# Layer 0's two gate chunks computed as 512-wide products

## The chip, the cores and the metric

The kernel runs on one core of a Trainium2 chip. The metric is the device time of one execution in microseconds (us); the median of three timed runs of the kernel before is 246.11 us (246.09 to 246.35). The profile is of a further execution of its own.

## The reference

Two layers run over 256 positions of width 1024, followed by a final RMSNorm. Each layer projects the normed input through one wide matrix, runs three kinds of heads on slices of the projection, multiplies each result by its own SiLU gate, and projects back:

```python
hn = rms_norm(x, norm_gain)
proj = jnp.einsum('bsd,de->bse', hn, w_in)
a_q, a_k, a_v, a_g, b_x, b_g, c_q, c_k, c_v, c_g = jnp.split(proj, _in_split_points(), axis=-1)
...
y_a = dilated_attention(qa, ka, va) ... * jax.nn.silu(a_g)
y_b = rg_lru_branch(b_x, ...) * jax.nn.silu(b_g)
y_c = stick_breaking_attention(qc, kc, vc) ... * jax.nn.silu(c_g)
y = jnp.concatenate([y_a, y_b, y_c], axis=-1)
return x + jnp.einsum('bse,ed->bsd', y, w_out)
```

The change concerns `c_g` (the stick-breaking gate) and `b_g` (the recurrent gate) of the first layer: 256 columns of the projection each.

## The kernel before

**Precision.** The inputs are float32. Each operand of a projection is split into a rounded part and a rest, both in a reduced type: `whi`, `wlo` for a chunk of weights and `xh`, `xl` for the input, which lie side by side in `xx`, so that the 512 columns of one `xx[:, k]` are the 256 positions of `xh` and then those of `xl`. A product is taken as three: hi·hi, hi·rest and rest·hi. The split of weights is ScalarE's copy (L115, `whi`) and VectorE's subtraction (L117, `wlo`), four of each per chunk of 256 columns, prefetched from a ring of DMA tiles `st`.

**Two forms of the projection.** `proj_b` (L326) makes a chunk in two halves of 128 columns, each a contraction over eight blocks k. A chunk that is not in `PAIRED` goes through `mm3` (L225): 16 products of 256 columns with `whi` and 8 with `wlo` for each half, both halves summed into one PSUM bank. A chunk in `PAIRED` makes, for each half, eight 512-wide products of `whi` with `xh` and `xl` at once (L344) and eight 256-wide ones of `wlo` with `xh` (L341), in a bank for each half; its two 256-column parts are then added, ScalarE copying one to `low` (L347) and VectorE adding the other (L349). Before, layer 0 has only the two chunks of the dilated gate (`CH_AG`, `CH_AG + 1`) in that form; layer 1 has nearly all.

**A gate in layer 0.** The norm's factor is not yet in `xx` there, so `silu` (L428) first multiplies the sum by the row `rb` (L413, through `scaled`), then takes the sigmoid on ScalarE (L84, through `tab`) and multiplies on VectorE (L435). `emit_y` (L437) multiplies a head group's result by its gate and splits that into `yh` (ScalarE, L441) and `yl` (VectorE, L442) for the output projection.

**Order.** TensorE runs in the order in which the code is written (`manual_schedule`). On the other engines a scheduler places the instructions when the program is built, and each engine then runs its list strictly in order. Around the change TensorE does, in layer 0: the stick-breaking gate's chunk (`CH_CG`), the transposes of the first four dilated heads' probabilities (L489), the first half of the recurrent gate's chunk (`CH_BG`), then `third`: the gates' products of the recurrence (`lru_gates`, L601), the values of the stick-breaking and of the first dilated heads (L453) and the score products of the other four dilated heads (`dil_scores`, L542); then the second half of `CH_BG`, the two dilated gate chunks and the output projection.

**PSUM.** The pool `pp` has three banks for projections, the pool `at` four banks named `s`, and `yp` one. Both rings give out the bank that was given out longest ago and is free again. So the four score banks of `dil_scores(4)` follow three banks of transposes and the two banks of `lru_gates`: the third and the fourth score bank are those that ScalarE's sigmoids read, `rt` from the one and `it` from the other (L605, shown as L84 with `rt<-s` and `it<-s`). One of the three `pp` banks is held by the first dilated heads' values (L670) until they are multiplied by their gate (`emit_y` at L688), so the dilated gate's four half chunks alternate between the other two: the second chunk's first half needs the bank of the first chunk's first half, which is free after its addition (`agf<-pp,low`, L349).

Of the kernel before, what the change touches and what calls it, by code (L numbers as in the profile page):

```python
# [42 lines left out]

CH_AV, CH_CV, CH_CQ, CH_CK, CH_BX, CH_CG, CH_BG, CH_AG, CH_O = 0, 2, 3, 4, 7, 10, 11, 12, 14
CH_AQ, CH_AK = (5, 8), (6, 9)
PAIRED = ((CH_AG, CH_AG + 1), (CH_CQ, CH_CK, CH_AQ[0], CH_AK[0], CH_BX, CH_AQ[1], CH_AK[1], CH_CG, CH_BG, CH_AG, CH_AG + 1))


@with_exitstack
def trunk_kernel(ctx: ExitStack, tc: tile.TileContext, x, first_x, first, wpack, prm_d, gatew, gains, consts, rope, out):  # L50
# [12 lines left out]
    def bank(pool, tag):  # L63
        return pool.tile([P, 512], F32, name=tag, tag=tag)

    def scr(w):
        return wk.tile([P, 512], F32, name="scr", tag="scr", bufs=SCR)[:, 0:w]
# [9 lines left out]
    def table(name, behind=()):  # L77
        load = act.preload_act_table_set(name)  # L78
        for u in (*loaded["users"], *behind):
            dep(load, u)  # L80
        loaded["load"], loaded["users"] = load, []

    def tab(*a, **k):
        i = dep(act.activation(*a, **k), loaded["load"])  # L84
        loaded["users"].append(i)
        return i

    def v2(a, n=2):
        return a.rearrange("p (b t) -> p b t", b=n)
# [34 lines left out]
    def ask(l, c, ahead=AHEAD):  # L124
        last = order.index((l, c)) + ahead
        while pending and order.index(pending[0]) <= last:
            i = pending.pop(0)
            ready[i] = load_chunk(*i)

    def weights(l, c, ahead=AHEAD):  # L130
        ask(l, c, ahead)
        return ready.pop((l, c))
# [87 lines left out]
    def mm3(ps, lhs, rhs, ks, first, last, skip=False):  # L220
        lh, ll = lhs
        rh, rl = rhs
        seq = [(a, b, k) for a, b in ((lh, rh), (lh, rl), (ll, rh)) for k in ks]
        for i, (a, b, k) in enumerate(seq):
            pe.matmul(ps, a(k), b(k), start=first and i == 0, stop=last and i == len(seq) - 1,  # L225
                      skip_group_check=skip)
# [84 lines left out]
    for l in range(L):  # L311
# [5 lines left out]
        def y_half(h):  # L317
            ys[h] = [sb.tile([P, 4, S], F32R, name=n, tag=f"{n}{h}") for n in ("yh", "yl")]
# [7 lines left out]
        def proj_b(c, mid=None, to=None, sc=1.0):  # L326
            pair = c in PAIRED[l]
            hi, lo = [a.rearrange("p (k c) -> p k c", c=256) for a in weights(l, c, AHEAD - 1 if mid else AHEAD)]
            if pair:
                flat = None if to is not None else scr(512)  # L330
                to = [v2(flat)[:, b, :] for b in range(2)] if to is None else to
            else:
                flat = bank(pp, "pp")
            for b in range(2):
                cs = slice(b * P, b * P + P)
                if pair:
                    ps = last["bank"] = bank(pp, "pp")
                    seq = [(b ^ i, k) for i in range(2) for k in range(NK)]
                    for i, (is_lo, k) in enumerate(seq):
                        if is_lo:  # L340
                            pe.matmul(ps[:, 0:S], lo[:, k, cs], xh[:, k, :], start=i == 0, stop=i == len(seq) - 1,  # L341
                                      skip_group_check=True)
                        else:
                            pe.matmul(ps, hi[:, k, cs], xx[:, k].rearrange("p h t -> p (h t)"), start=i == 0,  # L344
                                      stop=i == len(seq) - 1, skip_group_check=True)
                    low = wk.tile([P, S], F32, name="low", tag="low", bufs=2)
                    act.activation(low, ps[:, S:2 * S], AF.Copy, scale=sc)  # L347
                    if sc == 1.0:
                        dve.tensor_add(to[b], ps[:, 0:S], low)  # L349
                    else:  # L350
                        dve.scalar_tensor_tensor(to[b], ps[:, 0:S], sc, low, ALU.mult, ALU.add)
                else:
                    mm3(flat[:, b * 256:(b + 1) * 256], [lambda k, a=a: a[:, k, cs] for a in (hi, lo)],
                        [lambda k, a=a: a[:, k, :] for a in (xh, xl)], range(NK), b == 0, True, True)
                if b == 0 and mid:
                    mid()
                    ask(l, c)
            return flat

        def proj_to(dst, c, mid=None, sc=1.0):  # L360
            if l > 0 and c in PAIRED[l]:
                proj_b(c, mid, [dst[:, b, :] for b in range(2)], sc)
            else:
                scaled(dst, proj_b(c, mid), sc)

        def rows(ps, b=2):
            return v2(ps, b), rb.rearrange("p (o t) -> p o t", o=1).broadcast_to([P, b, S])
# [42 lines left out]
        def scaled(dst, ps, sc=1.0):  # L410
            if l == 0:
                a, b = rows(ps)
                dve.scalar_tensor_tensor(dst, a, sc, b, ALU.mult, ALU.mult)  # L413
            else:
                act.activation(dst, v2(ps), AF.Copy, scale=sc)
# [4 lines left out]
        def tables():  # L420
            if l == 0:
                nc.sync.dma_start(out=rp, in_=rope)
            nc.sync.dma_start(out=gw_t, in_=gatew[:, l, :])

        if l > 0:
            tables()

        def silu(dst, ps):  # L428
            sg = v2(scr(512))
            src = v2(ps)  # L430
            if l == 0:
                src = v2(scr(512))
                scaled(src, ps)
            tab(sg, src, AF.Sigmoid)
            dve.tensor_mul(dst, src, sg)  # L435

# [128 lines left out]
        def dil_transposes(h0):  # L565
            if h0 == 0:
                a = sb.tile([P, 1024], F32, name="pa", tag="yh1")
                b = sb.tile([P, 512], F32, name="pb", tag="yl1")
                to, heads = (a[:, 0:512], a[:, 512:1024], b), by_head(a, b)
            else:  # L570
                to, heads = turned_tile()
            turned(prob, h0, range(3), to)
            return heads
# [7 lines left out]
        bg = sb.tile([P, 2, S], F32, name="bg", tag="bg")  # L581
        cg = sb.tile([P, 2, S], F32, name="cg", tag="cg")
# [74 lines left out]
        rotated(CH_AK[1], kT, 4, "k1")  # L657
        split_qk(4, ("q0", "ag"))
        table(SIGM)
        cg_ps = proj_b(CH_CG)  # L660
        pts = dil_transposes(0)
        silu(cg, cg_ps)


        y_half(0)

        def third():
# [2 lines left out]
            y_c["y"] = values(va, pts, 0, bank(pp, "pp"))  # L670
            y_c["s"] = dil_scores(4)

        silu(bg, proj_b(CH_BG, third))
        y_half(1)
        table(LN_EXP)
        lru_scan()
# [2 lines left out]
        ps = None  # L679
        if CH_AG in PAIRED[l]:  # L680
            agf = sb.tile([P, 2, S], F32, name="agf", tag="cg")
            proj_b(CH_AG, None, [agf[:, b, :] for b in range(2)])
            ps = agf.rearrange("p b t -> p (b t)")
        dil_softmax(y_c["s"])
        ps = proj_b(CH_AG) if ps is None else ps
        table(SIGM)
        silu(ag[:, 0:2, :], ps)
        emit_y(y_c["y"], ag[:, 0:2, :], 4, 2)  # L688
        seeded = proj_b(CH_AG + 1)
        silu(ag[:, 2:4, :], seeded)  # L690
        if CH_AG + 1 in PAIRED[l]:
            seeded = last["bank"]
# [161 lines left out]
```

## Time and profile before

| | us |
|---|---|
| median of the timed runs | 246.11 |
| time of the profiled execution | 246.06 |
| span of its trace | 244.2 |
| TensorE busy, matmuls | 236.2 (97%) |
| TensorE busy, weight loads | 206.6 (85%) |
| VectorE busy | 200.0 (82%) |
| ScalarE busy | 174.4 (71%) |
| GpSimd busy | 10.5 (4%) |

Matmuls overlap in the trace, so a matmul's own duration is longer than its distance from the next; the steps of the chain of waits give the distance. Of the engines' instructions, too, the next one starts a little before the end of the one ahead. A name such as `whi<-st` says what an instruction writes and reads; L115 is line 115 of the kernel before. Times in the views count from the start of the span.

### The profile page before, as it was taken

To read this page: it belongs to the slowest core of one execution; us is meant where nothing else is said; L and a number is where in the kernel's file an instruction comes from. 1 tells how busy PE (TensorE), PEld (TensorE's weight loads), DVE (VectorE), ACT (ScalarE), POOL (GpSimd) and SP (SyncE) were. 2 spreads that over 40 slices of the span, in tenths; PEclk is the share of its full clock that TensorE was granted. 3 is DMA by queue.
4 is the path that set the end of the run, shared out by engine and by line. 5 is a ranking of instruction groups with operands and counts; after the bars stand their busy time and mean duration, and the time that the engine had idled before them with its cause. 6 is when DMAs were issued, how large, how long until landed. Compare 5 with 4: busy or idle time off the path is not lost.

```text
span 244.2 us, 4576 instructions
## 1 busy us (share of the span) xinstructions
PE 236.2 (97%) x1651; PEld 206.6 (85%) x1651; DVE 200.0 (82%) x480; ACT 174.4 (71%) x384; POOL 10.5 (4%) x43
## 2 busy tenths in 40 slices
PE   8799999999999999999999999999999999999991
PEld 4588999999999798878888888888888878887881
DVE  3694699999999889999495585999999986997362
ACT  3677987919597689994673674876669867998143
POOL 0017200002000000000000000000010000000000
PEclk9999999999999999999999999999999999999999
DMA  6989988565846843068448288615470771000022
GB/s 193 377 254 390 384 268 291 190 205 177 240 152 207 272 153 105 1 195 320 175 134 273 88 289 268 199 44 177 171 214 7 226 282 63 31 0 0 3 75 97
DMA packets 14037, 43.89 MB, mean 180 GB/s; under 512 B 1728, under 2 KB 3008, under 8 KB 14016
## 3 DMA queue, kind: packets, MB, share of 16 engines
q1 hardware_dynamic: 13248, 42.43, 51.9%
q0 software_dynamic: 192, 0.52, 0.8%
q10 hardware_dynamic: 576, 0.66, 0.7%
q8 instruction: 13, 0.21, 0.4%
q14 instruction: 8, 0.07, 0.1%
HBM read 42.03 MB, written 1.05 MB: 176 GB/s over the span
## 4 chain that ended last, share of the span: by engine, by line
PE 94%; DMA 3%; DVE 1%; SPq 0%; ACT 0%; issue 0%; DVEq 0%
PE pp L225 34%; PE pp L344 20%; PE pp L341 10%; PE s L225 9%; PE s L181 4%; PE s L489 3%; DMA st<-first 3%; PE y L453 2%; PE pp L383 2%; PE s L542 2%; PE pp L181 2%; PE s L469 1%; PE y L225 1%; PE pp L453 1%; PE s L601 1%; PE s L273 1%
## 5 line engine op out<-in xcount | busy, mean ns | idle before, releaser
L117 DVE TENSOR_TENSOR wlo<-st,whi 128x512 fp32r<-128x512 f32 x128 | 81.8, 684 | 7.5 <-ACT whi L115 6.9
L115 ACT ACTIVATE whi<-st 128x512 fp32r<-128x512 f32 x130 | 72.5, 627 | 9.0 <-DMA st<-w_pack 3.4
L344 PE MATMUL pp<-xx,whi 128*128 128x512 f32 x208 | 50.8, 393 | 0.0
L344 PEld LDWEIGHTS pp<-xx,whi 128*128 128x128 f32 x208 | 37.8, 188 | 7.6 <-DVE q L349 0.3
L225 PE MATMUL pp<-xx,whi 128*128 128x256 f32 x288 | 38.2, 285 | 0.0
L225 PEld LDWEIGHTS pp<-xx,whi 128*128 128x128 f32 x288 | 35.8, 191 | 0.8 <-issue 0.3
L341 PEld LDWEIGHTS pp<-xx,wlo 128*128 128x128 f32 x208 | 26.9, 191 | 1.6 <-ACT scr L84 0.3
L341 PE MATMUL pp<-xx,wlo 128*128 128x256 f32 x208 | 28.0, 284 | 0.0
L225 PE MATMUL pp<-xx,wlo 128*128 128x256 f32 x144 | 20.2, 283 | 0.0
L84 ACT ACTIVATE pr<-scr,mn 128x128 f32<-128x128 f32 (+1 forms) x32 | 14.1, 443 | 6.6 <-DVE mn L549 6.6
L225 PEld LDWEIGHTS pp<-xx,wlo 128*128 128x128 f32 x144 | 18.6, 192 | 0.0
L78 ACT ACT_TABLE_LOAD x13 | 16.7, 1283 | 1.9 <-PEq L847 1.7
L347 ACT ACTIVATE low<-pp 128x256 f32<-128x256 f32 x26 | 9.4, 373 | 8.8 <-PE pp L344 8.0
L225 PE MATMUL pp<-whi,yh 128*128 128x512 f32 (+1 forms) x48 | 14.1, 382 | 0.0
L225 PE MATMUL pp<-wlo,yh 128*128 128x512 f32 (+1 forms) x48 | 13.7, 372 | 0.0
L225 PE MATMUL pp<-whi,yl 128*128 128x512 f32 (+1 forms) x48 | 13.6, 371 | 0.0
L181 PE MATMUL s<-whi,xx 128*128 128x512 f32 (+1 forms) x36 | 9.6, 384 | 1.8 <-ACT xx L161 1.7
L225 PEld LDWEIGHTS pp<-whi,yl 128*128 128x128 f32 x48 | 8.6, 188 | 1.6
L225 PEld LDWEIGHTS pp<-wlo,yh 128*128 128x128 f32 x48 | 8.6, 188 | 1.6
L225 PEld LDWEIGHTS pp<-whi,yh 128*128 128x128 f32 x48 | 8.3, 188 | 1.6 <-issue 0.3
L549 DVE CUSTOM_DVE_ANT_0 scr<-s,con 128x128 f32<-128x128 f32 (+1 forms) x32 | 9.2, 350 | 0.0
L181 PEld LDWEIGHTS s<-whi,xx 128*128 128x128 f32 x36 | 6.0, 197 | 3.3 <-ACT xx L161 2.5
(189 smaller groups left out, 372.3 us busy)
## 6 DMA issues: line engine op xcount, KB each, us to landing
st<-w_pack SPq DMA_DIRECT2D x66, 512.0 KB, 5.3
st<-first SPq DMA_DIRECT2D x7, 512.0 KB, 7.0
xres<-x_in SPq DMA_DIRECT2D x4, 256.0 KB, 7.5
gw_t<-gate_w SPq DMA_DIRECT2D x2, 256.0 KB, 6.8
gn<-gains SPq DMA_DIRECT2D x2, 256.0 KB, 5.9
xs<-xc POOLq DMA_DIRECT2D x4, 128.0 KB, 3.8
gf<-gains SPq DMA_DIRECT2D x2, 256.0 KB, 5.4
out<-st ACTq DMA_DIRECT2D x2, 192.0 KB, 2.0
```

What stands on the lines that cost most here:

```text
L78: load = act.preload_act_table_set(name)
L84: i = dep(act.activation(*a, **k), loaded["load"])
L115: split[l, c] = act.activation(h, part, AF.Copy)
L117: dve.tensor_sub(r, part, h.bitcast(F32))
L181: pe.matmul(ps[t][:, c0:c1], a[:, k, t * P:(t + 1) * P], b, start=k == 0 and all(m[0] is not ps for m in seq[:i]), stop=k == NK - 1 and al ...
L225: pe.matmul(ps, a(k), b(k), start=first and i == 0, stop=last and i == len(seq) - 1, skip_group_check=skip)
L341: pe.matmul(ps[:, 0:S], lo[:, k, cs], xh[:, k, :], start=i == 0, stop=i == len(seq) - 1, skip_group_check=True)
L344: pe.matmul(ps, hi[:, k, cs], xx[:, k].rearrange("p h t -> p (h t)"), start=i == 0, stop=i == len(seq) - 1, skip_group_check=True)
L347: act.activation(low, ps[:, S:2 * S], AF.Copy, scale=sc)
L453: pe.matmul(y[hr, p * 128 + o:p * 128 + 256], vt[:, s0, hs], wts[i][s0], start=s0 == 0, stop=s0 == 1)
L489: pe.transpose(tp[:, i * P:(i + 1) * P], tiles[h0 + h][:, j * P:(j + 1) * P], ident)
L549: dve.tensor_tensor_reduce(xs[:, cs], sps[h][:, cs], nmask[:, cs], -0.125, 3e38, ALU.add, ALU.min, mn[:, t:t + 1])
```

## The change

The two gate chunks of layer 0 join `PAIRED`, and their halves are added straight into the gates' own tiles `cg` and `bg`, from which `silu` then reads.

```diff
-PAIRED = ((CH_AG, CH_AG + 1), (CH_CQ, CH_CK, ...
+PAIRED = ((CH_CG, CH_BG, CH_AG, CH_AG + 1), (CH_CQ, CH_CK, ...
...
+        def home(tile_):
+            return [tile_[:, b, :] for b in range(2)] if l == 0 else None
+
         def silu(dst, ps):
             sg = v2(scr(512))
-            src = v2(ps)
+            src = dst if ps is None else v2(ps)
             if l == 0:
-                src = v2(scr(512))
-                scaled(src, ps)
+                ps, src = src, v2(scr(512))
+                scaled(src, ps.rearrange("p b t -> p (b t)"))
             tab(sg, src, AF.Sigmoid)
             dve.tensor_mul(dst, src, sg)
...
-        cg_ps = proj_b(CH_CG)
+        cg_ps = proj_b(CH_CG, None, home(cg))
...
-        silu(bg, proj_b(CH_BG, third))
+        silu(bg, proj_b(CH_BG, third, home(bg)))
```

Per chunk, TensorE's 48 products of 256 columns become 16 of 512 and 16 of 256. ScalarE gets two copies more (L347) and VectorE two additions more (L349); the product with `rb` now reads `cg` or `bg` instead of PSUM. Each half has a bank of its own. Behind the edited lines all line numbers are 3 higher after the change (L435 becomes L438, and so on).

How the rows of the other engines move shows at three places. VectorE, from the split of the second dilated key tile (`qk`) to the first gated result; before:

```order
L528 TENSOR_TENSOR qk_1038<-k_965,qk_1038 128x512
L117 TENSOR_TENSOR wlo<-st,whi 128x512 x4
L413 SCALAR_TENSOR_TENSOR scr<-pp,rb 128x512
L117 TENSOR_TENSOR wlo<-st,whi 128x512 x3
L435 TENSOR_TENSOR cg<-scr 128x512
L117 TENSOR_TENSOR wlo<-st,whi 128x512
L615 TENSOR_TENSOR it<-it,xc 128x512
L439 TENSOR_TENSOR scr<-y,cg 128x512
```

And the same stretch after the change:

```order
L531 TENSOR_TENSOR qk_1038<-k_965,qk_1038 128x512
L349 TENSOR_TENSOR cg<-pp,low 128x256
L117 TENSOR_TENSOR wlo<-st,whi 128x512 x4
L349 TENSOR_TENSOR cg<-pp,low 128x256
L117 TENSOR_TENSOR wlo<-st,whi 128x512
L413 SCALAR_TENSOR_TENSOR scr<-cg,rb 128x512
L117 TENSOR_TENSOR wlo<-st,whi 128x512
L438 TENSOR_TENSOR cg<-scr 128x512
L117 TENSOR_TENSOR wlo<-st,whi 128x512 x2
L349 TENSOR_TENSOR bg<-pp,low 128x256
L618 TENSOR_TENSOR it<-it,xc 128x512
L442 TENSOR_TENSOR scr<-y,cg 128x512
```

Two additions and one subtraction of weights now stand ahead of the product with `rb` (L413) that feeds the sigmoid.

ScalarE from the copies of the transposed probabilities (`pa`, `pb`) to the dilated gate's first `low`, before (the first `scr<-scr` is the sigmoid of `cg`, the second that of `bg`):

```order
L490 ACTIVATE pb<-s 128x512
L84 ACTIVATE scr<-scr 128x512
L115 ACTIVATE whi<-st 128x512
L84 ACTIVATE rt<-s,prm_t 128x256 x2
L84 ACTIVATE it<-s,prm_t 128x256 x2
L84 ACTIVATE th<-rt,nc_286 128x256 x2
L441 ACTIVATE yh<-scr 128x512
L115 ACTIVATE whi<-st 128x512 x4
L84 ACTIVATE scr<-scr 128x512
L78 ACT_TABLE_LOAD
L84 ACTIVATE av<-rt,c_285 128x256 x2
L347 ACTIVATE low<-pp 128x256
```

And from the sigmoid of `cg` on after it:

```order
L84 ACTIVATE scr<-scr 128x512
L115 ACTIVATE whi<-st 128x512 x2
L347 ACTIVATE low<-pp 128x256
L84 ACTIVATE rt<-s,prm_t 128x256 x2
L84 ACTIVATE it<-s,prm_t 128x256 x2
L84 ACTIVATE th<-rt,nc_286 128x256 x2
L444 ACTIVATE yh<-scr 128x512
L347 ACTIVATE low<-pp 128x256
L115 ACTIVATE whi<-st 128x512 x3
L84 ACTIVATE scr<-scr 128x512
L78 ACT_TABLE_LOAD
L84 ACTIVATE av<-rt,c_285 128x256 x2
```

Between the sigmoid of `cg` and `rt` stand two copies of weights and one `low` instead of one copy of weights; ahead of the sigmoid of `bg` a `low` takes the place of one copy of weights.

VectorE again, where the first dilated heads' result is gated, ahead of the output projection; before:

```order
L442 TENSOR_TENSOR yl<-scr,yh 128x512
L435 TENSOR_TENSOR ag<-scr 128x512
L585 MEMSET bxp 128x2x3
L439 TENSOR_TENSOR scr<-pp,ag 128x512
L349 TENSOR_TENSOR scr<-pp,low 128x256 x2
```

After the change:

```order
L445 TENSOR_TENSOR yl<-scr,yh 128x512
L438 TENSOR_TENSOR ag<-scr 128x512
L117 TENSOR_TENSOR wlo<-st,whi 128x512
L442 TENSOR_TENSOR scr<-pp,ag 128x512
L349 TENSOR_TENSOR scr<-pp,low 128x256 x2
```

A subtraction of weights stands where the small memset was.

More of the change, by code (lines that the diff above doesn't have):

```diff
@@ L45 @@
 CH_AQ, CH_AK = (5, 8), (6, 9)
-PAIRED = ((CH_AG, CH_AG + 1), (CH_CQ, CH_CK, CH_AQ[0], CH_AK[0], CH_BX, CH_AQ[1], CH_AK[1], CH_CG, CH_BG, CH_AG, CH_AG + 1))
+PAIRED = ((CH_CG, CH_BG, CH_AG, CH_AG + 1), (CH_CQ, CH_CK, CH_AQ[0], CH_AK[0], CH_BX, CH_AQ[1], CH_AK[1], CH_CG, CH_BG, CH_AG, CH_AG + 1))
 @with_exitstack
```

## The prediction

> **What bounds the kernel now.** I read the page first: how busy each engine is, then the chain of waits.
>
> ```profile
> PE 236.2 (97%) x1651; PEld 206.6 (85%) x1651; DVE 200.0 (82%) x480; ACT 174.4 (71%) x384; POOL 10.5 (4%) x43
> PE 94%; DMA 3%; DVE 1%; SPq 0%; ACT 0%; issue 0%; DVEq 0%
> ```
>
> TensorE (PE) is busy for 97% of the span and makes up 94% of the chain that ends last. So a shorter TensorE stream shortens the kernel one for one, as long as nobody makes TensorE wait; and whoever does adds his lateness one for one. Next I read the chain in order of time around the two gates (start, length, what, and the number of matmuls).
>
> ```profile
> 60.12 14.59 PE pp L225 x120
> 74.71 1.31 PE s L489 x12
> 76.02 2.86 PE pp L225 x24
> 78.88 1.02 PE s L601 x16
> ...
> 82.66 1.36 PE s L542 x38
> 84.02 3.06 PE pp L225 x24
> 87.08 1.84 PE pp L344 x8
> 88.92 1.91 PE pp L341 x16
> ...
> 102.29 5.48 PE pp L225 x24
> ```
>
> The stick-breaking gate's chunk is the last 48 of the 120 matmuls in the first row. The recurrent gate's halves are the rows at 76.02 and 84.02; between them lie the recurrence's gate products at 78.88 and, last, the scores of four heads at 82.66. No other engine shows in this stretch: TensorE never waited. What I need, then, is how near the others come to being late. These are VectorE's rows in the order of time (start, length, line, what; in brackets the idle time ahead):
>
> ```profile
> 75.23 0.68 DVE L528 TENSOR_TENSOR qk<-k,qk 128x512 fp32r<-128x512 f32 x1
> 75.83 2.49 DVE L117 TENSOR_TENSOR wlo<-st,whi 128x512 fp32r<-128x512 f32 x4
> 78.24 0.68 DVE L413 SCALAR_TENSOR_TENSOR scr<-pp,rb 128x512 f32<-128x512 f32 x1
> ...
> 81.85 0.68 DVE L615 TENSOR_TENSOR it<-it,xc 128x512 f32<-128x512 f32 x1
> 82.45 0.68 DVE L439 TENSOR_TENSOR scr<-y,cg 128x512 f32<-128x512 f32 x1
> 83.83 0.69 DVE L442 TENSOR_TENSOR yl<-scr,yh 128x512 fp32r<-128x512 f32 x1 [0.70 <-ACT yh L441]
> ...
> 87.12 0.69 DVE L413 SCALAR_TENSOR_TENSOR scr<-pp,rb 128x512 f32<-128x512 f32 x1 [0.38 <-PE pp L225]
> ...
> 91.13 0.69 DVE L617 TENSOR_TENSOR scr<-av 128x512 f32<-128x512 f32 x1 [0.31 <-ACT av L84]
> 91.74 0.42 DVE L349 TENSOR_TENSOR agf<-pp,low 128x256 f32<-128x256 f32 x1
> ...
> 100.09 0.69 DVE L439 TENSOR_TENSOR scr<-pp,ag 128x512 f32<-128x512 f32 x1
> ```
>
> VectorE works without a gap from 75.23 to the product with rb at 78.24: whatever is put ahead of that product delays it. ScalarE in the same stretch:
>
> ```profile
> 79.02 0.63 ACT L84 ACTIVATE scr<-scr 128x512 f32<-128x512 f32 x1 [0.64 <-DVE scr L413]
> 79.55 0.61 ACT L115 ACTIVATE whi<-st 128x512 fp32r<-128x512 f32 x1
> 80.07 0.82 ACT L84 ACTIVATE rt<-s,prm_t 128x256 f32<-128x256 f32 x2
> 80.79 0.83 ACT L84 ACTIVATE it<-s,prm_t 128x256 f32<-128x256 f32 x2
> ...
> 88.26 0.61 ACT L84 ACTIVATE scr<-scr 128x512 f32<-128x512 f32 x1
> 88.89 1.28 ACT L78 ACT_TABLE_LOAD   x1
> 90.19 0.91 ACT L84 ACTIVATE av<-rt,c 128x256 f32<-128x256 f32 x2
> 91.00 0.36 ACT L347 ACTIVATE low<-pp 128x256 f32<-128x256 f32 x1
> ```
>
> The sigmoid at 79.02 is what the reader should look at. ScalarE stood idle for 0.64 us because VectorE's L413 was not done, with rt and it queued behind. it ends at 80.79 + 0.83 = 81.62 and frees the bank that the fourth head's scores are written to; TensorE comes there at 82.66. The slack is 1.04 us.
>
> **What TensorE saves.** The 120 matmuls at 60.12 begin behind another kind of product; such a restart costs 3.06 - 2.86 = 0.20 us by the two rows of the recurrent gate. So a half of 24 products takes (14.59 - 0.20)/5 = 2.88 us. A half in the new form takes eight wide products, 1.84 us by the row at 87.08, and eight narrow ones, half of the 1.91 at 88.92: 2.80 us. That saves 0.08 per half, **0.33 us** in four halves (unrounded 0.083 each). Three of the halves, 0.25 us, lie ahead of the scores.
>
> One rule bears on this. The Trainium skill ("TensorE: Matmul & The Clock Gate", section "Back-to-back issue gap") gives an isolated matmul's gap as N/2.4 + 2.5 ns, an estimated 216 ns for 512 columns and 109 for 256; by it a half would go from 24 x 109 = 2.62 us to 2.60, and the whole change would save TensorE 0.07 us, with a time 0.26 us above mine. The rows show 1.84/8 = 230 and 1.91/16 = 119 ns, so this trace does not bear the page out, and the sum goes by the rows.
>
> **What VectorE and ScalarE add ahead of the scores.** Nothing upstream moves, so VectorE ends the split of the key tile as before and is free at 75.83 (an instruction starts 0.08 us before the end of the one ahead: 75.23 + 0.68 against 75.83). Its new order puts ahead of L413 two additions of 0.42 - 0.08 = 0.34 us (the row at 91.74 is the same operation) and one more subtraction of weights at (78.24 - 75.83)/4 = 0.60: 1.28 us. The copies to low that the additions need stand on ScalarE where its rows had 0.64 us of idle time and one weight copy more, so they don't delay them. L413 starts at 79.52 and the sigmoid at 79.02 + 1.28 = 80.30. Reading the gate's tile instead of PSUM may make L413 itself a little quicker or slower; no row around it suggests more than 0.05.
>
> Between that sigmoid and rt stand now two weight copies and a low, where one copy stood. A copy takes 80.07 - 79.55 = 0.52; a low takes 0.36 - 0.10 = 0.26, since ScalarE starts the next instruction 0.10 early (79.02 + 0.63 against 79.55). So rt and it come 1.28 + 0.52 + 0.26 = 2.06 us later, and it ends at 83.68.
>
> TensorE reaches the scores at 82.66 - 0.25 = 82.41, may start the first two heads, and stands at the fourth head's first product. With about 0.05 us for the signal it goes on at 83.73, some 1.3 us after its arrival; the products of the first two heads that it has done already take off up to 0.07. I take **1.25 us**. This wait is not in the trace of before, so its ends: it is no less than 0.9 us if the placement on both engines costs 0.2 less on each, and no more than 1.6 if a weight tile or the signal comes late. Queued behind the waiting matmul is all the rest of TensorE's list, so the wait is paid in full. The DMAs issue from the SP queue in the same order as before and their tiles are wanted later, not earlier.
>
> **What comes next at the dilated gate.** The recurrent gate's second half ends at 87.08 - 0.33 + 1.25 = 88.00. Its low copy on ScalarE starts at 88.04 (VectorE's row at 87.12 shows 0.04 from the end of the matmuls to the reader). Then three weight copies follow: 88.04 + 0.26 + 1.56 = 89.86. VectorE meanwhile goes from it at 83.70 through the product with xc (0.60), the gated result (1.38 from 82.45 to 83.83, with ScalarE's yh between), yl (0.60) and the score reductions, 2.30 us from 83.83 + 0.61 to 87.12 - 0.38, where VectorE fell idle: 88.58. Its addition and L413 end at 88.58 + 0.34 + 0.68 = 89.60, in time for the sigmoid at 89.86. From there the row at 88.26 and those after it give 91.00 - 88.26 = 2.74 us to the dilated gate's low, which starts at 92.60. VectorE is held by the exponentials av until 92.73 (91.13 against 91.00), then does L617 (0.61) and the addition from 93.34 to 93.76. That addition frees the bank that TensorE needs after the two halves of the dilated gate's first chunk: 88.00 + 2 x 2.80 = 93.59. So TensorE waits **0.2 us** more. In the trace of before the same addition ended at 92.16, and TensorE came at 87.08 + 2 x 2.80 = 92.67: a slack of 0.5 us, of which the delay of VectorE relative to TensorE takes all. I keep 0 and 0.6 as ends.
>
> The other things moved I cost at nothing. The weight splits that fall behind are far ahead of their use: the four subtractions at 75.83 are of the second dilated gate chunk, which TensorE reaches at 92.67, so 2 us of delay there are covered by some 14. Were that cover gone, each would cost its 0.60.
>
> **The sum.** -0.33 + 1.25 + 0.2 = +1.12 us, against the profiled execution: its span of 244.2 us, and 1.86 around it, make 246.06. Forecast 247.18, say **247.2 us**, slower by 0.45%. The profiled execution is 0.05 below the median of 246.11, within the spread of the runs.
>
> **The rivals.**
>
> *No wait, only the shorter stream (not slower).* If it is done by the time TensorE comes, 82.45, the change gives its 0.33 us: 245.7. That decides at 0.83 us of added delay on VectorE and ScalarE together, where I count 2.06. For it speaks only that 1.04 us of slack stood there; against it, that VectorE had no gap to take the additions and that ScalarE was already waiting for it. 0.08.
>
> *Half of the delay.* If only VectorE's 1.28 us reach the bank (ScalarE makes up its part), it ends at 82.90, TensorE waits 0.5, and the second place keeps its slack: -0.33 + 0.5 = 246.2, within what can be told from no change. 0.10.
>
> *A third wait, at the output projection.* The gated first heads (VectorE's row at 100.09) hold a bank that TensorE wants at 102.29. It ends at 100.78: a slack of 1.5 us. After the change VectorE is 1.60 later (93.34 against 91.74), and has one subtraction more ahead of that product, 0.60: 102.98, against TensorE's 102.29 + 1.12 = 103.41. The 0.4 us that are left are less than the errors of this chain of steps. If it turns out 1 us longer, the time is 247.8. 0.15.
>
> *The wide products are no faster here.* Each form takes 2.88 us, because the restarts between short groups eat the gain. Then TensorE comes 0.25 later to the first wait and finds it that much shorter, and the sum is about 1.0 + 0.2 = 1.2: 247.3: not to be told from my forecast, and with it in the chances.
>
> **How the numbers follow.** The forecast with both waits, 246.8 to 247.6, has 0.63; the third wait 0.15, half of the delay 0.10, no wait 0.08, and 0.04 is for what I don't see. The range runs from 246.2 (half of the delay) to 247.9 (third wait and the upper end of the first); it leaves out the case without a wait and the tails, 0.15 or so. A measurement of this kernel can tell about 0.2%, 0.5 us, from no change. So slower, above 246.6, takes the forecast, the third wait and a little of the half: 0.81. Within 0.2% lie the half and the shorter stream alone, whose 0.33 us is 0.13%: 0.16. Faster by more than that would need over 0.5 us and TensorE has only 0.33 to give: 0.03.
>
> **What the profile after would show.** In the chain the row of scores begins with a step through ScalarE's it (a wait of 1.0 to 1.4 us); the sigmoid of cg starts near 80.3 and it ends near 83.7; a half of a gate takes 2.80 us in L344 and L341. A shorter wait on VectorE's addition stands ahead of the second dilated gate chunk. It would be wrong if it ends before 82.5, or if TensorE loses more than 0.6 us anywhere behind 95 us.

## The result, and the profile after

| | before | after |
|---|---|---|
| median | 246.23 us (245.68 to 246.36) | 247.64 us (247.18 to 248.35) |
| ratio, 95% interval | | 1.0071 [1.0047, 1.0094] |
| profiled execution, its span | 246.06, 244.2 | 247.71, 245.4 |
| TensorE: start of the stick-breaking gate's chunk to the first product of the output projection | 29.30 | 30.90 |
| from there to the end of the last matmul | 141.06 | 141.03 |

The kernel is slower by 0.7%: 1.75 us by the ratio (1.16 to 2.32). (The range of before leaves out one execution of 1327 us.) The median is 0.4 us above the forecast of 247.2, and inside the range that was given with it. The last two rows, each from one profiled execution, show where it went: TensorE loses 1.60 us between the first gate chunk and the output projection, and nothing behind it. That is what the steps have to account for; the spans differ by only 1.2, because the profiled execution of after came to the chunk 0.34 us earlier (68.44 against 68.78). The granted clock of TensorE was 0.999 in the execution of before and 0.995 in that of after; since the 141 us behind the output projection's start agree to 0.03, it is not the cause.

The page of after, its line of busy times and the shares of the chain that ends last:

```profile
PE 236.7 (96%) x1619; PEld 205.2 (84%) x1619; DVE 201.2 (82%) x484; ACT 175.4 (71%) x388; POOL 11.1 (5%) x43
PE 74%; DVE 13%; ACT 7%; DMA 2%; issue 1%; SPq 0%; DVEq 0%; ACTq 0%
```

TensorE has 32 matmuls fewer (1651 before) and yet is not less busy. The chain, which was TensorE for 94%, now runs through VectorE and ScalarE for a fifth of the span. The chain in the order of time shows why (start, length, what):

```profile
75.51 0.40 DVE cg L349
75.91 2.40 DVE wlo L117 x4
78.31 0.34 DVE cg L349
78.65 0.60 DVE wlo L117
79.24 0.61 DVE scr L413
...
80.48 1.14 ACT whi L115 x2
81.61 0.27 ACT low L347
81.88 0.41 ACT rt L84 x2
...
82.49 0.85 ACT it L84 x2
...
83.39 1.42 PE s L545 x29
...
88.22 1.56 ACT whi L115 x3
89.78 0.52 ACT scr L84
...
90.32 1.28 ACT L78
...
91.62 0.92 ACT av L84 x2
...
92.56 0.69 DVE scr L620
93.25 0.34 DVE agf L349
...
93.64 2.11 PE pp L344 x8
```

Read it from the bottom. TensorE's row at 93.64 (the second dilated gate chunk) is released by VectorE's addition `agf`, which comes behind ScalarE's exponentials `av`. TensorE's row at 83.39 (the scores) is released by `it`. Ahead of `it` stand, one behind the other, the items that the prediction named: two additions to `cg`, one more split of weights, then on ScalarE two copies and a `low`. So there are two places where TensorE waits. Here is TensorE's own timeline from the start of the first gate chunk to the output projection (start, length, line, operands, count; in brackets the idle time ahead), first of before:

```profile
68.78 2.08 PE L225 MATMUL pp<-xx,whi 128*128 128x256 f32 x16
...
82.59 0.73 PE L542 MATMUL s<-k,q 32*128 32x128 f32 x16
...
83.95 2.17 PE L225 MATMUL pp<-xx,whi 128*128 128x256 f32 x16
...
90.67 3.82 PE L344 MATMUL pp<-xx,whi 128*128 128x512 f32 x16
...
98.08 0.62 PE L225 MATMUL s<-whi,yh 128*128 128x512 f32 x2
```

and of after:

```profile
68.44 2.00 PE L344 MATMUL pp<-xx,whi 128*128 128x512 f32 x8
...
74.04 1.48 PE L492 MATMUL s<-con,pr 128*128 128x128 f32 x12
75.28 2.09 PE L344 MATMUL pp<-xx,whi 128*128 128x512 f32 x8
...
82.03 1.11 PE L545 MATMUL s<-k,q 32*128 32x128 f32 x6
83.39 0.50 PE L545 MATMUL s<-k,q 32*128 32x128 f32 x8 [0.25 <-ACT it L84]
...
84.74 1.22 PE L341 MATMUL pp<-xx,wlo 128*128 128x256 f32 x8
...
91.36 2.00 PE L344 MATMUL pp<-xx,whi 128*128 128x512 f32 x8
93.64 2.11 PE L344 MATMUL pp<-xx,whi 128*128 128x512 f32 x8 [0.27 <-DVE agf L349]
...
99.34 0.62 PE L225 MATMUL s<-whi,yh 128*128 128x512 f32 x2
```

From the first score product to the second half of the recurrent gate are 83.95 - 82.59 = 1.36 us before and 84.74 - 82.03 = 2.71 after: **the first wait costs 1.35 us**. The bracket at 83.39 shows only 0.25, since much of the wait lies inside the row ahead of it, in which six products take 1.11 us where sixteen took 0.73; start against start is the safe reading. From the second half of the recurrent gate to the output projection are 14.13 us before and 14.60 after. With 0.08 saved in that half, **the second wait costs 0.55**. And from the start of the first chunk to the second half are 15.17 before (83.95 - 68.78) and 16.30 after (84.74 - 68.44): 1.35 more for the wait, and 0.22 saved in three halves. -0.22 + 1.35 - 0.08 + 0.55 = +1.60.

### The profile page after: what moved, and what is told of

It reads as the page before. It is cut to its first block, busy times and chain, and to the rows that moved or that the text cites. A ratio compares the mean times of both kernels' runs of the same rounds, so it can differ in the third digit from the quotient of the medians.

```text
span 245.4 us, 4518 instructions
## 1 busy us (share of the span) xinstructions
PE 236.7 (96%) x1619; PEld 205.2 (84%) x1619; DVE 201.2 (82%) x484; ACT 175.4 (71%) x388; POOL 11.1 (5%) x43
## 4 chain that ended last, share of the span: by engine, by line
PE 74%; DVE 13%; ACT 7%; DMA 2%; issue 1%; SPq 0%; DVEq 0%; ACTq 0%
PE pp L344 19%; PE pp L225 18%; PE pp L341 10%; PE s L225 9%; DVE wlo L117 5%; PE s L181 4%; DMA st<-first 2%; PE pp L383 2%; PE s L492 2%; ACT whi L115 2%; PE pp L181 2%; PE y L456 2%; PE s L545 2%; ACT pr L84 1%; DVE sw L483 1%
## 5 line engine op out<-in xcount | busy, mean ns | idle before, releaser
L344 PE MATMUL pp<-xx,whi 128*128 128x512 f32 x240 | 59.0, 393 | 0.3 <-DVE agf L349 0.3
L344 PEld LDWEIGHTS pp<-xx,whi 128*128 128x128 f32 x240 | 43.5, 188 | 9.3 <-DVE agf L349 0.9
L225 PE MATMUL pp<-xx,whi 128*128 128x256 f32 x224 | 29.5, 285 | 0.0
L225 PEld LDWEIGHTS pp<-xx,whi 128*128 128x128 f32 x224 | 27.8, 192 | 0.5 <-issue 0.3
L347 ACT ACTIVATE low<-pp 128x256 f32<-128x256 f32 x30 | 10.8, 373 | 11.3 <-PE pp L344 10.5
L483 DVE TENSOR_TENSOR_SCAN sw<-scr,con 128x127 f32<-128x127 f32 (+1 forms) x16 | 7.9, 537 | 1.1 <-ACT scr L84 1.1
```

Source lines behind the costliest of these rows:

```text
L483: dve.tensor_tensor_scan(w[:, lo:lo + n][:, ::-1], om[:, lo + 1:lo + 1 + n][:, ::-1], diag[:, 255 - n:255][:, ::-1], 0.0, ALU.mult, ALU.add)
```

## The experiments

All variants compute the same sums; only late4 makes copies that are overwritten. Two numbers serve for each, both from one profiled execution: TensorE's way from the start of the stick-breaking gate's chunk to the output projection (29.30 us before, 30.90 after) and from there to the end of the last matmul (141.06 and 141.03). These are the steps. The stretch behind the output projection came out within 0.03 us in after and in six of the nine variants, so differences of 0.1 us can be read in them; the time of an execution scatters by more. The table has all of them, as differences from before; the times are relative to runs of before on the same chip.

| kernel | to the output projection | behind it | time, ratio [95%] |
|---|---|---|---|
| after | +1.60 | -0.03 | 1.0071 [1.0047, 1.0094] |
| rt_first | +0.68 | -0.02 | 1.0044 [1.0031, 1.0058] |
| ag_first | +1.02 | +0.22 | 1.0065 [1.0051, 1.0078] |
| rt_ag_first | -0.32 | +0.68 | 1.0034 [1.0018, 1.0050] |
| narrow | +1.68 | -0.02 | 1.0097 [1.0080, 1.0113] |
| cg_only | +0.87 | 0.00 | 1.0031 [1.0012, 1.0050] |
| bg_only | +0.41 | -0.02 | 1.0021 [0.9999, 1.0043] |
| late4 | +1.58 | -0.02 | 1.0072 [1.0051, 1.0094] |
| bg_late | +0.70 | 0.00 | 1.0036 [1.0016, 1.0055] |
| bg_late2 | +0.30 | +0.29 | 1.0052 [1.0027, 1.0076] |

**Take the first wait away (rt_first).** The sigmoid of `cg` is placed behind `rt` and `it` on ScalarE, so that the score banks come free without it.

```diff
-        silu(cg, cg_ps)
+        if l > 0:
+            silu(cg, cg_ps)
...
             lru_gates()
+            if l == 0:
+                silu(cg, cg_ps, last["it"])
```

(`silu`'s third argument makes its sigmoid stand behind `it` in ScalarE's order.)

> The changed kernel with the sigmoid of cg put behind rt and it on ScalarE (same operations, one of them moved). Theory of the two waits: it ends near 81.1 us, before TensorE comes to the scores near 82.0, so the first wait (1.35 us of TensorE in the profile after) is gone; the second, before the dilated gate's second chunk, stays (about 0.5 us with the restart). Time 1.35 below the changed kernel's: about 246.3, the kernel before within 0.3. Rival, the wide products themselves or their banks make TensorE slower: the time stays near 247.6. Rival, a later wait takes over what is gained: between, and another row of waits in the profile.

The first wait is gone: 14.95 us from the first chunk to the second half of the recurrent gate, 0.22 less than before, which is the saving of three halves. But the second wait grew from 0.55 to 1.0 us, so that of the 1.35 only 0.92 came back. The chain of rt_first up to the waiting matmul:

```profile
87.90 0.35 DVE bg L349
...
89.06 0.63 ACT scr L84
...
89.71 1.28 ACT L78
...
91.00 0.92 ACT av L84 x2
...
91.95 0.69 DVE scr L622
92.64 0.34 DVE agf L349
...
93.03 2.11 PE pp L344 x8
```

TensorE is done with the products ahead of that wait at 92.32 (in after at 93.36), 1.04 us sooner on the clocks of the two traces, but the addition `agf` ends at 92.98 (93.59), only 0.61 sooner: on VectorE the sum of `bg` stands behind the score reductions until 87.90, and the sigmoid of `bg`, the table load, `av` and `agf` follow it.

**Take the second wait away (ag_first), and both (rt_ag_first).** The recurrence's exponentials and scan are written behind the dilated gate's first chunk, so `low` and `agf` no longer stand behind `av`.

```diff
-        table(LN_EXP)
-        lru_scan()
-        emit_y(rt, bg, 2, 2)
+        if l > 0:
+            ...
             ps = agf.rearrange("p b t -> p (b t)")
+        if l == 0:
+            table(LN_EXP)
+            lru_scan()
+            emit_y(rt, bg, 2, 2)
```

> The changed kernel with the dilated gate's first copy and addition put ahead of the recurrence's exponentials av and the product L617 that waits for them. Theory of the two waits: the addition that frees the bank ends about 1.1 us earlier, so TensorE no longer waits for it; the wait for it at the scores stays at 1.3. Time about 0.5 below the changed kernel's: 247.1. Rival, the second wait is not worth its 0.5 because later slack takes it up: 247.6.

> Both moves at once in the changed kernel. Theory of the two waits: TensorE waits nowhere in layer 0 and only the shorter stream is left, 0.3 below the kernel before: 245.8, and 1.8 below the changed kernel. Rival, the wide products make TensorE slower: 247 or more. Rival, delays of VectorE and ScalarE reach the output projection (yh, yl or the bank of the first dilated heads) once TensorE runs ahead again: 246.2 to 246.8 with a new wait near 100 us.

In ag_first the way to the output projection is +1.02: the first wait, 1.35, less the whole saving, 0.33; the second wait is gone. In rt_ag_first both are gone, and TensorE comes to the output projection 0.32 us sooner than before. This is the saving alone, 0.33 by the prediction. But it is more than given back behind: +0.68 from there to the end, as the last rival in the run's expectation had it. TensorE's timeline in rt_ag_first:

```profile
97.69 0.61 PE L225 MATMUL s<-whi,yl 128*128 128x512 f32 x2
98.22 0.73 PE L225 MATMUL s<-whi,yh 128*128 128x512 f32 x2
98.80 0.62 PE L225 MATMUL s<-wlo,yh 128*128 128x512 f32 x2
99.61 0.73 PE L225 MATMUL s<-whi,yl 128*128 128x512 f32 x2 [0.19 <-DVE yl L447]
```

The steps between such rows are 0.45 us where nothing waits (97.69 - 97.24); here they are 0.53, 0.58 and 0.81. TensorE waits at the output projection for the gated recurrent heads, `yh` and `yl`, whose place on VectorE and ScalarE has moved back. Part of this was there for ag_first, +0.22.

**Same orders, narrow products (narrow).** The rounded weights are multiplied with `xh` and `xl` apart, as before the change, everything else as after it.

```diff
+                        elif l == 0 and c in (CH_CG, CH_BG):
+                            for h, part in enumerate((xh, xl)):
+                                pe.matmul(ps[:, h * S:h * S + S], hi[:, k, cs], part[:, k, :], ...)
                         else:
                             pe.matmul(ps, hi[:, k, cs], xx[:, k]..., ...)
```

> The changed kernel, its banks, copies, additions and orders, but each 512-wide product of the two gate chunks made as two 256-wide ones with the same weights (xh, then xl). Theory of the two waits: TensorE comes 0.25 later to the scores and waits that much less, and loses the 0.08 that the last half saved: 247.7, as the changed kernel within 0.2. Rival, the wide products are what costs: back at 246.1.

+1.68, against +1.60 with wide products; and both waits are there, on the same engines. So the loss doesn't come from TensorE's new products: with the old ones in the new orders it is as large. Of the products' saving of 0.33 only 1.68 - 1.60 = 0.08 is seen in after, one half chunk's, since TensorE that arrives sooner at the scores waits longer.

**One chunk each (cg_only, bg_only).** Only one of the two gates joins `PAIRED`; the diff is that of cg_only, and bg_only has `CH_BG` in place of `CH_CG`. The other gate keeps its old call of `silu`.

```diff
-PAIRED = ((CH_CG, CH_BG, CH_AG, CH_AG + 1), ...
+PAIRED = ((CH_CG, CH_AG, CH_AG + 1), ...
```

> Only the stick-breaking gate's chunk in the new form; the recurrent gate's as before. Theory of the waits: the two additions and the weight split still stand ahead of the sigmoid of cg, and one more weight copy behind it, so it comes 1.28 + 0.52 = 1.80 us later than before, TensorE 0.17 earlier, and the wait at the scores is about 0.95 us; no second wait, since the recurrent gate has no copy ahead of its sigmoid. From the start of the stick-breaking gate to the output projection 29.30 - 0.17 + 0.95 = 30.1 us, time 0.8 above the kernel before. Rival, the two chunks cost alike (the form itself): half of the whole, 0.7 each.

> Only the recurrent gate's chunk in the new form. Theory of the waits: the sigmoid of cg starts as before, near 79.0, only one low copy (0.26) stands between it and rt, so it ends 0.8 us before TensorE comes and the first wait is gone; the second wait, for the dilated gate's first addition, is there with 0.5. From the start of the stick-breaking gate to the output projection 29.30 - 0.17 + 0.5 = 29.6 us, time 0.3 above the kernel before. Rival, the two chunks cost alike: 0.7 above.

cg_only has the first wait alone: two halves save 0.16, +0.87 remains, so the wait is 1.03. The 0.32 that it lacks against 1.35 is the `low` of `bg` on ScalarE (0.26 in the prediction) and TensorE's arrival, 0.08 later. bg_only has the second wait alone: -0.16 + 0.57 = +0.41. The second wait is thus not a consequence of the first. The two runs together give 0.87 + 0.41 = 1.28, not 1.60: the 0.32 between them is what the second gate adds to the first wait. Half of the whole for each, the rival, did not come.

**Delay alone (late4).** The kernel before, with four copies of 128x512 on ScalarE between the sigmoid of `cg` and `rt`; they write `rt`, which the sigmoid then overwrites.

```diff
+            for _ in range(4 if l == 0 else 0):
+                dep(act.activation(rt, v2(va[:, 0, :]), AF.Copy), last["sig"])
             for g, dst in ((0, rt), (1, it)):
```

> The kernel before, with four copies of 512 columns (va to rt, overwritten afterwards) put on ScalarE between the sigmoid of cg and rt: 2.08 us, as much as the change delays it, with TensorE's products untouched. Theory of the waits: slack 1.04, so TensorE waits 1.05 at the scores, and 29.30 becomes 30.35; time 1.0 above the kernel before. Rival, a delay of rt and it is not what costs (the products do): 246.1 as before.

A wait of 1.58 us came, at the same products. ScalarE's timeline in late4:

```profile
79.25 0.63 ACT L84 ACTIVATE scr<-scr 128x512 f32<-128x512 f32 x1 [0.72 <-DVE scr L413]
79.78 0.61 ACT L604 ACTIVATE rt<-va 128x512 f32<-128x512 f32 x1
80.30 0.62 ACT L115 ACTIVATE whi<-st 128x512 fp32r<-128x512 f32 x1
80.82 1.94 ACT L604 ACTIVATE rt<-va 128x512 f32<-128x512 f32 x3
82.79 0.84 ACT L84 ACTIVATE rt<-s,prm_t 128x256 f32<-128x256 f32 x2
83.52 0.84 ACT L84 ACTIVATE it<-s,prm_t 128x256 f32<-128x256 f32 x2
```

The last three copies take 0.66 us each, (82.79 - 80.82)/3, not the 0.52 of copies of weights, which go into different tiles. `it` ends at 84.36. With this execution's start 0.23 later (69.01 against 68.78), that is 2.51 later than the 81.62 of before; less the slack of 1.04, 1.47, and 0.05 from the end of `it` to the matmul at 84.41. The sum is 1.52, against 1.58 measured: delay less slack is what TensorE pays, and the slack of 1.04 us read from the trace of before holds to within 0.06. The delay of 2.51 is larger than the 2.08 expected, since the copies took longer, and this kernel has no second wait; that its +1.58 stands so near to the +1.60 of after is chance.

**The recurrent gate's sigmoid behind the dilated gate's first chunk (bg_late, bg_late2).** To lose neither bank: rt_first, and in addition `bg`'s sigmoid and the scan later, the `low` copies and additions forward; bg_late2 puts these further forward and loads the sigmoid table later.

```diff
-        silu(bg, proj_b(CH_BG, third, home(bg)))
+        proj_b(CH_BG, third, home(bg))
...
+        if l == 0:
+            table(LN_EXP)
+            lru_scan()
         dil_softmax(y_c["s"])
         ...
+        if l == 0:
+            silu(bg, None)
+            emit_y(rt, bg, 2, 2)
```

> The changed kernel with all three waits taken out by order alone: the sigmoid of cg behind it, the recurrent gate's sigmoid moved behind the exponentials and the square root (so that the chain av, Ln, Exp, scan starts some 3 us earlier), and the dilated gate's copy and addition ahead of Ln and of the product behind it. Theory of the waits: only the shorter stream is left, 29.30 - 0.32 = 29.0 us from the gate to the output projection, and nothing added behind it; time 0.3 below the kernel before. Rival, the moved work makes a new wait in the dilated gate (its copies now stand behind exponentials): 246.2 or more.

> As the run with bg's sigmoid behind the dilated gate's first chunk, but the low copy and the addition of the recurrent gate's second half stand one head earlier among the softmax rows, and the sigmoid table is loaded behind the last low of the dilated gate's first chunk, with its addition ahead of the scan. Theory (banks freed late are the only cost): no wait is left in the dilated gate, from the chunk of cg to the output projection 29.0 us (0.3 less than before), from there to the end 141.05; ratio near 0.999, to be told from 1 only just. Rival (whatever is moved early makes something else late, at the latest at the output projection): 29.0 but 0.3 us or more behind it, or a wait of 0.3 at another place of the stretch; ratio 1.000 to 1.003.

bg_late: nothing is lost behind the output projection, but in the dilated gate two other waits came. TensorE's timeline:

```profile
87.61 2.44 PE L341 MATMUL pp<-xx,wlo 128*128 128x256 f32 x16
...
95.05 1.22 PE L341 MATMUL pp<-xx,wlo 128*128 128x256 f32 x8 [0.39 <-DVE agf L349]
```

The first is a wait for the addition to `bg`, inside a group that takes 2.44 instead of 2.08; the second is for `agf`, whose `low` stood behind the table load on ScalarE until 94.20, and which itself stood behind a scan on VectorE until 94.59. By starts they cost 0.37 and 0.65 us, and -0.32 + 0.37 + 0.65 = +0.70. In bg_late2 the second shrank to 0.27, but the first stayed at 0.36, though its `low` now came in time. From the chain of bg_late2:

```profile
87.61 0.61 DVE scr L626
...
88.25 0.69 DVE scr L627
88.94 0.34 DVE bg L349
...
89.33 1.22 PE pp L341 x8
```

The addition stands behind two products of the recurrence on VectorE, as it did in bg_late; and behind the output projection 0.29 are lost again, in the steps ahead of products that read `yh` and `yl`. Both rivals came true, then: each order that was tried trades one wait for another, and no variant is faster than the kernel before (bg_only can't be told from it). Whether an order exists that keeps the 0.33 is open.

## Where the prediction was right, and the step that failed

The forecast was +1.12 us; the steps show +1.60, the times +1.75 by the ratio and +1.41 by the medians. Direction, places and causes were right. The step that failed is the price of the second wait, whose restart the prediction put at nothing; the price of the first was a little too small.

**TensorE's saving, -0.33: right.** rt_ag_first shows -0.32 where nothing waits, and in after's first chunk a half takes (74.04 - 68.44)/2 = 2.80 us, as predicted. By the gap that the Trainium skill ("TensorE: Matmul & The Clock Gate", section "Back-to-back issue gap") gives for an isolated matmul, N/2.4 + 2.5 ns, four halves would save an estimated 0.08 us (eight products fewer in each half, 2.5 ns for each; the prediction has 0.07, from rounded gaps); the 0.32 of rt_ag_first does not bear it out.

**The first wait, 1.25: right in place and cause, 0.10 too small.** By the prediction L413 starts at 79.52, the sigmoid at 80.30, and `it` ends at 83.68. The row of VectorE's timeline in after, and two of ScalarE's:

```profile
79.16 0.69 DVE L413 SCALAR_TENSOR_TENSOR scr<-cg,rb 128x512 f32<-128x512 f32 x1
```

```profile
79.94 0.63 ACT L84 ACTIVATE scr<-scr 128x512 f32<-128x512 f32 x1 [2.46 <-DVE scr L413]
...
82.49 0.84 ACT L84 ACTIVATE it<-s,prm_t 128x256 f32<-128x256 f32 x2
```

They are at 79.16, 79.94 and 82.49 + 0.84 = 83.33: each 0.35 or 0.36 early, as the whole stretch is in this execution (0.34). So the chain of steps was right to 0.02 us. What the prediction took off for products that were already done (0.07) was not there: in the chain of after the 29 products from 83.39 on take 1.42 us, where all 38 took 1.36 before.

**The second wait, 0.2: this is the term that was mis-sized; it measured 0.55.** The place, the bank and its releaser are as predicted. In the prediction the step is "So TensorE waits 0.2 us more", the lateness alone, 93.76 - 93.59 = 0.17. In TensorE's rows of after, above, the products ahead end at 91.36 + 2.00 = 93.36, and the addition at 93.59 (93.25 + 0.34): a lateness of 0.23, nearly as predicted (with the 0.34 of this execution, TensorE comes 0.11 and the addition 0.17 later than in the prediction). To it come 0.05 from there to the first matmul, and a part that the prediction had no term for: the eight products behind the wait take 2.11 us in the chain instead of 1.84. Of these 0.27, 0.16 is the head start that is lost: where nothing waits, TensorE's row of a group starts 2.00 - 1.84 = 0.16 before the end of the one ahead. The other 0.11 is a longer group, 2.11 us from start to end against the 2.00 at 91.36; such a group is not special to a wait, as the one at 75.28, which follows another kind of product without waiting, takes 2.09. 0.23 + 0.05 + 0.27 = 0.55. The same 2.11 stands in rt_first behind a longer wait, where 0.66 of lateness, 0.05 and 0.27 give the 0.98, so the restart does not grow with the wait's length; bg_only shows 0.57 for the second wait without the first.

**The sum.** With these two sizes -0.33 + 1.35 + 0.55 = +1.57, and +1.60 was measured, against +1.12 on record.

**The rivals.** *No wait* and *half of the delay* fell: the delay reached the bank in full, in after and in late4. *No faster wide products* fell by the -0.32 of rt_ag_first, but was right that the difference would hardly show in the time (narrow, +1.68 against +1.60). *A third wait at the output projection* did not come in after (141.03 behind it). It lay near: with the other two gone it was there, +0.68, but through the operands `yh` and `yl`, not through the bank that the prediction named.

**Open.** The times of the variants lie 0.3 us on average above what their steps give, from 0.1 below (cg_only) to 0.7 above (narrow, bg_late2). The steps come from one execution of each kernel, the times from four or more: rt_ag_first has +0.36 by steps and +0.84 in time, but its profiled execution, 245.85, is next to the shortest of twelve, whose median is 246.76. Part of the difference may lie ahead of the first gate chunk, where executions differ (below); no run settles it.

## What to carry to other kernels

When TensorE bounds a kernel and never waits, read the slack of the engine that frees its next bank before giving that engine anything: here a saving of 0.33 us on the bound engine brought 2.06 us of delay on a path with 1.04 us of slack. Price a new wait as lateness plus the restart of the pipeline behind it, which here was larger than the lateness. And after the removal of one wait look for the next: in rt_first, rt_ag_first and bg_late2 a following place took up a part of what was gained.

## What the runs showed of the hardware

- Behind a wait for a bank TensorE took 2.11 us for eight 512-wide products, where the chain without a wait has 1.84 (after, rt_first).
- Three copies on ScalarE that followed each other from one tile into one other took 0.66 us each, where copies of weights, each into a tile of its own, took 0.52 (late4). That the shared tile is the reason is not shown.
- A product of VectorE took the same from SBUF as from PSUM: L413 0.69 reading `cg`, 0.68 reading `pp` before.
- The input DMA with which the chain of waits begins varies from execution to execution: it took 6.25 us in before, 6.13 in after, 6.45 in rt_first and 5.46 in rt_ag_first, and the stick-breaking gate's chunk begins at 68.75 us in rt_first and at 67.80 in rt_ag_first. The row of rt_ag_first's chain (start, length, what):

```profile
1.64 5.46 DMA st<-first
```

That difference of 1.0 us is more than most of the effects here; comparisons by stage, start against start, are free of it.
